# A two-layer decoder trunk: feed-forward stages entered by halves of the tokens

## The chip, the cores and the metric

The kernel runs on one core of a Trainium2 chip. The metric is device time in microseconds. Before the change the median of three runs is 2155.39 us (2155.28 to 2158.04). One more execution was profiled; it took 2157.71 us.

## The reference

512 tokens of width 1024 pass two layers in float32. Every sub-layer reads a norm of the residual x and adds to x:

```
x = x + 1/2 * swiglu_ffn(rmsnorm(x, ffn1_norm[i]), ffn1_w_gu[i], ffn1_w_down[i])
x = x + mixer_i(rmsnorm(x, mix_norm[i]))     # i=0: RG-LRU and mLSTM ("ab"); i=1: sparse attention ("nsa")
x = x + 1/2 * swiglu_ffn(rmsnorm(x, ffn2_norm[i]), ffn2_w_gu[i], ffn2_w_down[i])
...
rmsnorm(x, g)   = x * rsqrt(mean(x*x) + EPS) * g
swiglu_ffn(x)   = (silu(x @ gate) * (x @ up)) @ w_down          # inner width D_FF = 2816
out             = rmsnorm(x, final_norm)
```

## The kernel before, in words

**Layout.** x stands transposed in eight tiles `X[0..7]` of 128 features x 512 tokens. Six stages follow each other: f0a, ab, f0b, f1a, nsa, f1b; the four named f are feed-forward stages (`ffn`, L310). Each float32 operand of TensorE is split in two, a rounded part (a copy on ScalarE, `hi`) and a remainder (a subtraction on VectorE, `lo`), and each product is three matmuls, L171 to L173 (`mm3`). Weights pass `wload` (L157 on): a DMA on SP's queue into one of two `raw` buffers, a copy into one of three `whi` (L165), a remainder into `wlo` (L166). Its instructions have a priority 90 places ahead of the program's order (`AHEAD`).

**A feed-forward stage** has 22 pairs, each 128 columns of gate and of up. Pairs 0 and 1 are done in full: 16 products of 512 tokens on the scaled but unnormed x (`prep`, L98, made by the stage before in its closing loop), with the norm's sums over features (`rms_sum`, L130) and its spread over partitions (`rms_row`, L142) in between. Then `quarters` (L240) makes the normed x (`xn`, L248), cuts it by halves of features and of tokens into B11, B12, B21, B22, and forms Q7, Q6, Q5, Q4 from them. The other 20 pairs (`pair`, L364) do seven products of a quarter instead of eight, 4 x 3 matmuls of 256 tokens each, with the weights summed alike on GpSimd (`sload`, L280 to L306; L289 to L292 are the sums, L303 and L304 copy and remainder, at a priority 230 ahead). They need three PSUM banks: `a` takes B11, then Q6, Q5 and B22 on top of each other, `e` takes Q7 and Q4, `b` B21. After each product its value is read: ScalarE L387, L389, L393, VectorE L395, L384, L380, then L374, L375, and `down` (L319) splits the result into `h`. The next product on the same bank waits for that reading. B22 of a pair is done after B11 and Q7 of the next (`left`).

After every eight pairs (the last time six) the down projection adds its eight output tiles to X (L412 to L421), 512 tokens at a time; in the last of these rounds, the closing, it calls `nxt` for each tile. The mixers close with their output projections, `out_proj` (L423) and `out_half(1)` in `nsa`. After f1b the final norm scales X and eight DMAs write it out (L1138 to L1141).

**Order.** `manual_schedule(engines=PE_ONLY)` keeps TensorE's instructions of a block as written. The other engines' queues, and tiles' places in the pools, are set by a list scheduler that takes ready instructions by priority: the place in the program less the offset given by `high_priority`. Blocks `b0` to `b16` of 2064 columns are shared by all stages under one tag each.

## Time and profile before

| | us |
|---|---|
| median of three runs | 2155.39 |
| profiled execution | 2157.71 |
| its span, first to last instruction | 2156.0 |
| TensorE busy | 2034.5 (94%) |
| VectorE busy | 1467.9 (68%) |
| ScalarE busy | 1040.1 (48%) |
| GpSimd busy | 876.8 (41%) |

PE is TensorE's matmul, PEld its weight load, DVE VectorE, ACT ScalarE, POOL GpSimd, SP the queue of the DMAs. Matmuls overlap, so one is shown longer (0.28 us for 256 columns) than the step from one start to the next. The chain that ended last lies on PE for 71% of the span and on DVE for 15%. `ps` and `pt` are PSUM tiles, `t` the tiles t1 and t2, `qB` and `qQ` the quarters of x, `r` the summed weights.

### The profile page before, as it was taken

The page shows a single profiled execution, that of the slowest core. Times are in us where ns is not written, and L with a number is a line of the kernel's source. Part 1 is how long each engine was busy: PE and PEld are TensorE (multiplying, and loading weights), DVE is VectorE, ACT ScalarE, POOL GpSimd, SP SyncE. Part 2 cuts the span into 40 slices and gives each one's busy share as a digit, 9 for nine tenths or more (in the row PEclk, how much of TensorE's full clock was granted, in tenths as well). Part 3 has the DMA queues.
Part 4 walks back from the last instruction along what each step waited for, and adds up shares of the span by engine and source line. Part 5 has one row for each costly group of instructions (what it writes and reads, how often), then busy time and mean ns, then how long its engine had stood idle before and what let it go on. Part 6 is the DMA issues. An engine that isn't in the chain of part 4 may idle for free.

```text
span 2156.0 us, 31290 instructions
## 1 busy us (share of the span) xinstructions
PE 2034.5 (94%) x12184; PEld 1772.0 (82%) x12184; DVE 1467.9 (68%) x2057; ACT 1040.1 (48%) x1876; POOL 876.8 (41%) x618
## 2 busy tenths in 40 slices
PE   6899999989997999999799999999999997999997
PEld 5789988867876989898698989877777676989896
DVE  7866847489566939576784858533777778848474
ACT  4434535355443525355452525424878754535252
POOL 6534522243222616254361625201655553526242
PEclk8899999999798999999899999999999998999998
DMA  4232322322121322323132332421000031323322
GB/s 158 69 100 97 118 74 69 103 69 79 68 98 59 108 85 98 107 89 111 51 108 88 108 93 89 126 87 70 30 21 16 31 103 59 108 88 108 93 67 76
DMA packets 75765, 182.13 MB, mean 84 GB/s; under 512 B 7393, under 2 KB 8161, under 8 KB 75617
## 3 DMA queue, kind: packets, MB, share of 16 engines
q1 hardware_dynamic: 75472, 180.06, 25.9%
q8 instruction: 95, 1.56, 0.3%
q14 instruction: 54, 0.43, 0.1%
q10 hardware_dynamic: 144, 0.09, 0.0%
HBM read 178.02 MB, written 2.10 MB: 84 GB/s over the span
## 4 chain that ended last, share of the span: by engine, by line
PE 71%; DVE 15%; issue 6%; ACT 5%; POOL 2%; DMA 1%; SPq 0%; POOLq 0%; ACTq 0%; DVEq 0%
PE ps L171 18%; PE ps L172 17%; PE ps L173 17%; PE pt L172 3%; DVE wlo L304 2%; PE pt L173 2%; PE pt L171 2%; PE px L945 2%; DVE t L375 2%; PE pt L740 2%; DVE xn L248 1%; ACT wx L303 1%; DVE wlo L166 1%; PE pt L961 1%; DVE qQ L258 1%
## 5 line engine op out<-in xcount | busy, mean ns | idle before, releaser
L289 POOL TENSOR_TENSOR r<-r,r 128x512 f32<-128x512 f32 x80 | 137.9, 1724 | 651.6 <-DMA r<-wgu 588.3
L165 ACT ACTIVATE whi<-raw 128x1024 fp32r<-128x1024 f32 (+2 forms) x180 | 176.7, 982 | 363.9 <-PE ps L172 249.3
L303 ACT ACTIVATE whi<-r 128x1024 fp32r<-128x1024 f32 x192 | 182.7, 952 | 236.1 <-PE ps L172 172.3
L304 DVE TENSOR_TENSOR wlo<-r,whi 128x1024 fp32r<-128x1024 f32 x192 | 254.6, 1328 | 54.4 <-ACT whi L303 52.6
L172 PE MATMUL ps<-h,whi 128*128 128x512 f32 x704 | 277.9, 395 | 0.0
L171 PE MATMUL ps<-h,whi 128*128 128x512 f32 x704 | 277.1, 394 | 0.0
L173 PE MATMUL ps<-h,wlo 128*128 128x512 f32 x704 | 276.6, 393 | 0.0
L419 DVE SCALAR_TENSOR_TENSOR X<-ps,X 128x512 f32<-128x512 f32 x96 | 66.4, 692 | 255.7 <-PE ps L173 255.7
L166 DVE TENSOR_TENSOR wlo<-raw,whi 128x1024 fp32r<-128x1024 f32 (+2 forms) x150 | 184.7, 1232 | 79.3 <-ACT whi L165 74.5
L304 DVE TENSOR_TENSOR wx<-r,wx 128x1024 fp32r<-128x1024 f32 (+1 forms) x128 | 185.7, 1451 | 51.2 <-ACT wx L303 49.6
L171 PE MATMUL ps<-qB,whi 128*128 128x256 f32 x576 | 166.4, 289 | 10.5 <-DVE t L380 10.5
L172 PE MATMUL ps<-qB,whi 128*128 128x256 f32 x576 | 163.8, 284 | 2.4 <-DVE qB L256 2.1
L173 PE MATMUL ps<-qB,wlo 128*128 128x256 f32 x576 | 163.3, 284 | 0.0
L303 ACT ACTIVATE wx<-r 128x1024 fp32r<-128x1024 f32 (+1 forms) x128 | 121.4, 948 | 80.8 <-PE pt L173 36.3
L172 PEld LDWEIGHTS ps<-h,whi 128*128 128x128 f32 x704 | 132.2, 188 | 31.5 <-DVE h L322 1.7
L171 PE MATMUL ps<-x,whi 128*128 128x512 f32 x368 | 154.6, 420 | 3.2 <-ACT whi L1094 3.2
L173 PEld LDWEIGHTS ps<-h,wlo 128*128 128x128 f32 x704 | 132.4, 188 | 30.7
L171 PEld LDWEIGHTS ps<-h,whi 128*128 128x128 f32 x704 | 132.2, 188 | 30.7
L112 POOL TENSOR_TENSOR acc<-acc,t 128x512 f32<-128x512 f32 x48 | 76.1, 1585 | 195.9 <-ACT t L110 190.8
L290 POOL TENSOR_TENSOR r<-r 128x512 f32<-128x512 f32 x80 | 146.1, 1826 | 17.2 <-DMA r<-wgu 17.1
L291 POOL TENSOR_TENSOR r<-r,r 128x512 f32<-128x512 f32 x80 | 150.6, 1883 | 5.8
L292 POOL TENSOR_TENSOR r<-r 128x512 f32<-128x512 f32 x80 | 147.0, 1837 | 6.1
(340 smaller groups left out, 6048.0 us busy)
## 6 DMA issues: line engine op xcount, KB each, us to landing
r<-wgu SPq DMA_DIRECT2D x80, 512.0 KB, 3.7
r<-wgu SPq DMA_DIRECT2D x160, 256.0 KB, 2.9
raw<-wd SPq DMA_DIRECT2D x64, 512.0 KB, 3.5
raw<-wd SPq DMA_DIRECT2D x32, 384.0 KB, 3.1
raw<-ab_fm SPq DMA_DIRECT2D x21, 512.0 KB, 3.3
raw<-nsa_fm SPq DMA_DIRECT2D x17, 512.0 KB, 3.3
raw<-wgu SPq DMA_DIRECT2D x14, 512.0 KB, 3.3
raw<-ab_out SPq DMA_DIRECT2D x8, 512.0 KB, 3.3
```

What stands on the lines that cost most here:

```text
L112: nc.gpsimd.tensor_add(acc, acc, sq)
L165: nc.scalar.activation(hi[:, :n], raw[:, :n], AF.Copy)
L166: (eng or nc.vector).tensor_sub(lo[:, :n], raw[:, :n], hi[:, :n].bitcast(F32))
L171: nc.tensor.matmul(ps, wh, xh, start=start, stop=False, skip_group_check=on)
L172: nc.tensor.matmul(ps, wh, xl, start=False, stop=False, skip_group_check=on)
L173: nc.tensor.matmul(ps, wl, xh, start=False, stop=stop, skip_group_check=on)
L289: nc.gpsimd.tensor_add(ra[:, 1], ra[:, 0], rc[:, 3])
L290: nc.gpsimd.tensor_add(rc[:, 1], rc[:, 0], rc[:, 3])
L291: nc.gpsimd.tensor_add(ra[:, 2], ra[:, 0], rc[:, 1])
L292: nc.gpsimd.tensor_add(rc[:, 2], ra[:, 3], ra[:, 2])
L303: nc.scalar.activation(hi[:, :m * T], src, AF.Copy)
L304: nc.vector.tensor_sub(lo[:, :m * T], src, hi[:, :m * T].bitcast(F32))
```

## The change

Stages f0b, f1a and f1b no longer start with two full pairs; their 22 pairs are all done by quarters. For that the sub-layer ahead of each closes by halves of the tokens: all eight output tiles for the first 256 tokens, then all eight for the other 256, each with its own `wload` (`closing`, `out_proj`, `out_prod`). After each half tile its square is summed (`square_half`). During the second half, after its third tile, the norm of the first half is formed and B11 and B21 with it (`mid`). The quarters of the second half are made as sums of others: Q7 from the unnormed difference times the norm's row in PSUM, Q6 from B11 and Q7, Q4 from B21 and Q6, Q5 and B22 on GpSimd (`second`). The first three pairs of such a stage run side by side, in the order written in `ffn`. f0a does three full pairs and makes its quarters the same way. The final norm is done by halves too. Readings of products get a priority of 320 (`EV`) or 160. Stages ab and nsa keep their full entry (`Rows`). The blocks of some tiles change places.

```diff
 AHEAD = 90
 SAHEAD = 230
+EV = 320
+H = T // 2
 PSB = 5
 NCMP = 31
 PE_ONLY = {mybir.EngineType.PE}
...
+        def square_half(i, t):
+            ts = slice(t * H, (t + 1) * H)
+            if i == 0:
+                nc.scalar.activation(acc[:, ts], X[i][:, ts], AF.Square)
+                return None
+            sq = tp.tile([P, T], F32, name="t2", bufs=3)[:, :H]
+            nc.scalar.activation(sq, X[i][:, ts], AF.Square)
+            if i < KT - 1:
+                nc.gpsimd.tensor_add(acc[:, ts], acc[:, ts], sq)
+            return sq
...
+        def rms_sum_half(t, sq):
+            ps = psum()
+            for c in range(2):
+                n = 2 * t + c
+                nc.tensor.matmul(ps[:, 2 * c:2 * c + 2], acc[:, n * P:(n + 1) * P], ones, start=True, stop=False)
+                nc.tensor.matmul(ps[:, 2 * c:2 * c + 2], sq[:, c * P:(c + 1) * P], ones, start=False, stop=True)
+            ms = tp.tile([P, NT], F32, name="ms")[:, :2]
+            root = tp.tile([P, NT], F32, name="root")[:, :2]
+            nc.scalar.activation(root, ps[:, 0:4:2], AF.Sqrt, scale=1.0 / D, bias=eps)
+            nc.vector.tensor_scalar(ms, ps[:, 0:4:2], 1.0 / D, EPS, op0=OP.mult, op1=OP.add)
+            rsqrt(Rcol[:, 2 * t:2 * t + 2], ms, root)
...
+            def tile(self, i, t):
+                self.sq[t] = square_half(i, t)
+                if t:
+                    self.early(i)
+            def early(self, i):
+                g, n = col(self.g, i), ng[:, PRM[self.g] + i:PRM[self.g] + i + 1]
+                if i < 4:
+                    nc.scalar.activation(self.xg[:, i], X[i][:, H:], AF.Copy, scale=g)
+                else:
+                    nc.vector.scalar_tensor_tensor(self.d7[:, i - 4], X[i][:, H:], n, self.xg[:, i - 4],
+                                                   op0=OP.mult, op1=OP.add)
...
+            def split(self, name, src, parts=1):
+                t = blk(self.qb[QS.index(name)], F32R, f"q{name}")
+                hi, lo = (t[:, n * 4 * H:(n + 1) * 4 * H].rearrange("p (k t) -> p k t", k=4) for n in range(2))
+                for n in range(parts):
+                    ks = slice(n * 4 // parts, (n + 1) * 4 // parts)
+                    nc.scalar.activation(hi[:, ks], src[:, ks], AF.Copy)
+                    nc.vector.tensor_sub(lo[:, ks], src[:, ks], hi[:, ks].bitcast(F32))
+                self.Q[name] = hi, lo
...
+            def first(self):
+                for i in range(KT):
+                    n = ng[:, PRM[self.g] + i:PRM[self.g] + i + 1]
+                    nc.vector.scalar_tensor_tensor((self.b11, self.b21)[i // 4][:, i % 4], X[i][:, :H], n, R[:, :H],
+                                                   op0=OP.mult, op1=OP.mult)
+                    if i == 3:
+                        self.split("B11", self.b11)
+            def mid(self):
+                with tc.high_priority(offset=60):
+                    rms_sum_half(0, self.sq[0])
+                    rms_row_half(0)
+                    self.first()
+                    self.split("B21", self.b21)
+            def second(self, row, parts):
+                f3 = blk(self.fb[2], F32, "qf3")[:, :4 * T].rearrange("p (s k t) -> p s k t", s=2, k=4)
+                q6, q4 = f3[:, 0], f3[:, 1]
+                for n in range(parts):
+                    ks = slice(n * 4 // parts, (n + 1) * 4 // parts)
+                    nc.vector.tensor_mul(self.d7[:, ks], self.d7[:, ks],
+                                         row.unsqueeze(1).to_broadcast([P, 4 // parts, H]))
+                nc.gpsimd.tensor_mul(self.xg, self.xg, R[:, H:].unsqueeze(1).to_broadcast([P, 4, H]))
+                self.split("Q7", self.d7, parts)
+                nc.vector.scalar_tensor_tensor(q6, self.b11, -1.0, self.d7, op0=OP.mult, op1=OP.subtract)
+                self.split("Q6", q6)
+                nc.gpsimd.tensor_add(self.b11, self.xg, self.b11)
+                nc.vector.scalar_tensor_tensor(q4, self.b21, -1.0, q6, op0=OP.mult, op1=OP.subtract)
+                self.split("Q4", q4)
+                nc.gpsimd.tensor_sub(self.xg, self.d7, self.xg)
+                self.split("Q5", self.b11)
+                self.split("B22", self.xg)
...
+        def closing(prod, upd, fin):
+            for t in range(2 if fin.halves else 1):
+                ts = slice(t * H, (t + 1) * H) if fin.halves else slice(0, T)
+                for i in range(KT):
+                    ps = psum()[:, :ts.stop - ts.start]
+                    prod(i, ps, ts)
+                    upd(i, ps, ts)
+                    fin.tile(i, t)
+                    if t and i == 2:
+                        fin.mid()
+        turns = [0, 0]
...
+        def quartered(w, rb):
+            ra, rc = (blk(rb[2 * (turns[1] % 2) + i], F32, f"r{i}")[:, :4 * T].rearrange("p (s c) -> p s c", s=4)
+                      for i in range(2))
+            turns[1] += 1
+            nc.sync.dma_start(ra[:, 0:4:3], w[0].rearrange("p (s c) -> p s c", s=2))
+            nc.sync.dma_start(rc[:, 3], w[1][:, :T])
+            nc.sync.dma_start(rc[:, 0], w[1][:, T:])
+            nc.gpsimd.tensor_add(ra[:, 1], ra[:, 0], rc[:, 3])
+            nc.gpsimd.tensor_add(rc[:, 1], rc[:, 0], rc[:, 3])
+            nc.gpsimd.tensor_add(ra[:, 2], ra[:, 0], rc[:, 1])
...
+        def into(jobs):
+            hi, lo = parts(len(jobs))
+            at = 0
+            for W, src, names in jobs:
+                cs = slice(at * T, (at + len(names)) * T)
+                src = src.rearrange("p s c -> p (s c)")
+                nc.scalar.activation(hi[:, cs], src, AF.Copy)
+                nc.vector.tensor_sub(lo[:, cs], src, hi[:, cs].bitcast(F32))
+                for name in names:
...
+            def load(self, w, rb):
+                with tc.high_priority(offset=SAHEAD):
+                    q = quartered(w, rb)
+                    for names in (("B11", "Q7"), ("Q6", "B21"), ("Q4", "Q5"), ("B22",)):
+                        if names[0] not in self.W and names[-1] not in self.W:
+                            into([(self.W, q[names if len(names) > 1 else names[0]], names)])
+                return self
...
+            def p1(self):
+                self.a, self.t1 = psum(), tp.tile([P, T], F32, name="t1", bufs=3)
+                self.product(self.a, "B11", True)
+                with tc.high_priority(offset=EV):
+                    nc.scalar.activation(self.t1[:, :H], self.a[:, :H], AF.Copy)
+            def p2(self):
+                b = psum()
+                self.product(b, "B21", True)
+                with tc.high_priority(offset=EV):
+                    nc.vector.tensor_add(self.t1[:, :H], b[:, :H], self.t1[:, :H])
+                nc.scalar.activation(self.t1[:, :H], self.t1[:, :H], AF.Silu, scale=-1.0)
+            def p7(self):
+                self.e, self.t2 = psum2(), tp.tile([P, T], F32, name="t2", bufs=3)
+                self.product(self.e, "Q7", True)
+                with tc.high_priority(offset=EV):
+                    nc.scalar.activation(self.t2[:, H:], self.e[:, :H], AF.Copy)
+            def p6(self):
+                self.product(self.a, "Q6", False)
+                with tc.high_priority(offset=EV):
+                    nc.scalar.activation(self.t2[:, :H], self.a[:, :H], AF.Copy)
+            def p4(self):
+                self.product(self.e, "Q4", False)
+                with tc.high_priority(offset=EV):
+                    nc.vector.tensor_add(self.t2[:, :H], self.e[:, :H], self.t2[:, :H])
+            def p5(self):
+                self.product(self.a, "Q5", False)
+                with tc.high_priority(offset=EV):
+                    nc.vector.tensor_add(self.t2[:, H:], self.a[:, :H], self.t2[:, H:])
+            def p3(self):
+                self.product(self.a, "B22", False)
+                with tc.high_priority(offset=EV):
+                    nc.scalar.activation(self.t1[:, H:], self.a[:, :H], AF.Silu, scale=-1.0)
+                with tc.high_priority(offset=EV // 2):
+                    nc.vector.tensor_mul(self.t2, self.t1, self.t2)
+                    self.down(self.t2)
...
+                start, at, wait = 3, 19, []
+                for j in range(start):
...
+                    if j == 1:
+                        for i in range(KT):
+                            quarters.early(i)
+                        quarters.first()
+                        for args in wait:
+                            j, t2 = hidden(*args)
+                            downs(j)(t2)
+                        wait.clear()
+                j, t2 = hidden(*wait[0])
+                quarters.split("B21", quarters.b21)
+                quarters.second(R[:, H:], 1)
+                downs(j)(t2)
+            else:
+                start = 3
+                pairs = {j: Pair(Q, downs(j)) for j in range(start)}
+                for p, j in ((pairs[j], j) for j in range(start)):
+                    hi, lo = wload(wgu[j, 0])
+                    p.W["B11"], p.W["B21"] = (hi[:, :T], lo[:, :T]), (hi[:, T:], lo[:, T:])
+                p0, p1, p2 = pairs.values()
+                with tc.high_priority(offset=SAHEAD):
+                    q0, q1 = quartered(wgu[0], rb), quartered(wgu[1], rb)
+                    for name in ("Q7", "Q6", "Q4", "Q5", "B22"):
+                        into([(p0.W, q0[name], (name,)), (p1.W, q1[name], (name,))])
+                    q2 = quartered(wgu[2], rb)
+                    for names in (("Q7", "Q6"), ("Q4", "Q5"), ("B22",)):
+                        into([(p2.W, q2[names if len(names) > 1 else names[0]], names)])
                 with tc.manual_schedule(engines=PE_ONLY):
+                    p0.p1()
+                    p0.p2()
+                    with tc.high_priority(offset=EV):
+                        rms_sum_half(1, quarters.sq[1])
+                    p1.p1()
+                    p1.p2()
+                    with tc.high_priority(offset=EV):
+                        row = rms_row_half(1)
+                        quarters.second(row, 2)
+                    p2.p1()
+                    p2.p2()
+                    for f in (p0.p7, p1.p7, p0.p6, p1.p6, p0.p4, p1.p4, p0.p5, p1.p5, p2.p7, p0.p3, p2.p6, p1.p3,
+                              p2.p4, p2.p5):
+                        f()
+                left = [p2.p3]
...
+                    for j in range(max(start, j0), j1):
+                        p = Pair(Q, downs(j)).load(wgu[j], rb)
+                        end = j == j1 - 1
+                        p.p1()
+                        p.p7()
+                        for f in left:
+                            f()
+                        p.p6()
+                        p.p2()
+                        if end:
+                            p.p5()
+                            p.p4()
+                            p.p3()
+                        else:
+                            p.p4()
+                            p.p5()
+                        left = [] if end else [p.p3]
...
+            closing(out_prod, lambda i, ps, ts: nc.vector.tensor_add(X[i][:, ts], ps, X[i][:, ts]), fin)
...
+            def tile(self, i, t):
+                ts = slice(t * H, (t + 1) * H)
+                self.sq[t] = square_half(i, t)
+                nc.vector.tensor_scalar(X[i][:, ts], X[i][:, ts], col("final_norm", i), None, op0=OP.mult)
+            def put(self, t):
+                ts = slice(t * H, (t + 1) * H)
+                rms_sum_half(t, self.sq[t])
+                ps = rms_row_half(t)
+                for i in range(KT):
+                    if i in (2, 4, 6):
+                        nc.gpsimd.tensor_mul(X[i][:, ts], X[i][:, ts], R[:, ts])
+                    else:
+                        nc.vector.tensor_mul(X[i][:, ts], X[i][:, ts], ps)
+                    nc.sync.dma_start(out[:, i, ts], X[i][:, ts])
+            def mid(self):
+                self.put(0)
...
+        qb = tuple(range(7))
+        lay = ((7, 8, 9, 10), (13, 14, 15, 16), (11, 12))
+        quarters = Quarters(plan["f0a"], qb, (10, 9, 8))
+        rows = Rows(plan["ab"], 0)
+        ffn(a["wgu"][0], a["wd"][0], x, quarters, lay, rows, first)
+        quarters = Quarters(plan["f0b"], qb, (10, 9, 8))
+        ab(rows.x, quarters)
+        following = Quarters(plan["f1a"], qb, (10, 6, 8))
+        ffn(a["wgu"][1], a["wd"][1], None, quarters, lay, following)
+        rows = Rows(plan["nsa"], 0)
+        ffn(a["wgu"][2], a["wd"][2], None, following, lay, rows)
+        quarters = Quarters(plan["f1b"], (4, 5, 6, 7, 14, 15, 16), (13, 12, 3))
+        nsa(rows.x, quarters)
+        end = Output()
+        ffn(a["wgu"][3], a["wd"][3], None, quarters, ((2, 3, 12, 13), (8, 9, 10, 11), (0, 1)), end)
+        end.put(1)
```

## Rows read from the trace of the kernel before

**Rows 1.** The page, part 1: busy time, share of the span, instructions.

```profile
PE 2034.5 (94%) x12184; PEld 1772.0 (82%) x12184; DVE 1467.9 (68%) x2057; ACT 1040.1 (48%) x1876; POOL 876.8 (41%) x618
```

**Rows 2.** Waits of TensorE, whole span: us in total, times, longest.

```profile
PE ps L171 <- DVE t L380: 22.7, 37, 1.8
...
PE pt L171 <- ACT qQ L254: 20.4, 7, 4.6
```

**Rows 3.** Stretches: busy time (instructions) of each engine, clock, DMA share, GB/s.

```profile
986.00:1019.20 33.20, 33.20 (x146) 27.05 (x145) 19.13 (x24) 18.30 (x26) 8.98 (x6) 1.00 0.31 95
644.70:668.70 24.00, 24.00 (x114) 19.81 (x112) 13.86 (x18) 8.14 (x10) 4.64 (x2) 1.00 0.15 44
1087.30:1098.68 11.38, 11.38 (x99) 11.38 (x97) 9.76 (x11) 6.34 (x11) 8.40 (x5) 1.00 0.34 116
596.40:644.70 48.30, 46.85 (x200) 37.82 (x199) 27.82 (x37) 22.09 (x32) 14.70 (x9) 0.96 0.31 101
596.40:751.10 154.70, 139.47 (x815) 123.94 (x814) 113.73 (x125) 73.84 (x110) 65.81 (x36) 0.92 0.26 84
986.00:1124.50 138.50, 124.50 (x763) 111.95 (x762) 103.42 (x112) 70.09 (x104) 60.65 (x33) 0.94 0.27 84
1742.30:1873.60 131.30, 115.76 (x722) 102.58 (x721) 107.88 (x118) 69.88 (x107) 65.42 (x37) 0.92 0.29 94
45.70:129.80 84.10, 65.94 (x505) 64.13 (x504) 75.33 (x72) 44.83 (x69) 46.76 (x26) 0.86 0.24 77
1169.00:1250.70 81.70, 80.29 (x673) 79.47 (x672) 67.51 (x69) 45.88 (x78) 55.85 (x32) 1.00 0.34 111
683.00:687.00 4.00, 4.00 (x21) 4.00 (x20) 4.00 (x4) 0.26 (x1) 2.76 (x3) 0.50 0.02 8
```

**Rows 4.** Quarters: VectorE remainder (min/median/max ns); ScalarE copy (busy us, mean ns).

```profile
L258 DVE TENSOR_TENSOR qQ<-qs,qQ x16: 1210/1748/2299, 56.4 to 1814.6; 128x1024 fp32r<-128x1024 f32 x16
...
L254 ACT ACTIVATE qQ<-qs 128x1024 fp32r<-128x1024 f32 x16 | 16.8, 1050 | 10.4 <-POOL qs L266 5.2 <-POOL qs L271 5.2
```

**Rows 5.** Timeline near 660 us: start us, us, engine, operation, count.

```profile
660.51 3.40 DVE L248 SCALAR_TENSOR_TENSOR xn<-X,prm,R 128x512 f32<-128x512 f32 x5 [1.04 <-ACT R L148]
...
663.17 3.55 DVE L248 SCALAR_TENSOR_TENSOR xn<-X,prm,R 128x512 f32<-128x512 f32 x2
...
663.33 2.84 POOL L266 TENSOR_TENSOR qs<-xn 128x1024 f32<-128x1024 f32 x1 [14.48 <-DVE xn L248]
```

**Rows 6.** Timeline of VectorE in the output projection: two remainders of one buffer.

```profile
612.39 1.22 DVE L166 TENSOR_TENSOR wlo<-raw,whi 128x1024 fp32r<-128x1024 f32 x1 [0.18 <-ACT whi L165]
...
618.04 1.25 DVE L166 TENSOR_TENSOR wlo<-raw,whi 128x1024 fp32r<-128x1024 f32 x1 [0.29 <-ACT whi L165]
```

**Rows 7.** DMA issues: count, KB each, median us to landing.

```profile
raw<-ab_out SPq DMA_DIRECT2D x8, 512.0 KB, 3.3
...
raw<-wd SPq DMA_DIRECT2D x32, 384.0 KB, 3.1
...
raw<-nsa_out SPq DMA_DIRECT2D x16, 256.0 KB, 2.7
```

**Rows 8.** ScalarE copy and VectorE remainder of a 768-column weight tile.

```profile
L165 ACT ACTIVATE whi<-raw 128x768 fp32r<-128x768 f32 x32 | 27.1, 847 | 43.0 <-PE ps L172 24.9 <-issue 12.2 <-PE pt L172 4.0
...
L166 DVE TENSOR_TENSOR wlo<-raw,whi x8: 957/958/1945, 982.2 to 1016.2; 128x768 fp32r<-128x768 f32 x6, 128x1024 fp32r<-128x1024 f32 x2
```

**Rows 9.** Waits of TensorE from 668.7 to 751.1 us.

```profile
PE pt L171 <- ACT qQ L254: 5.0, 2, 2.8
...
PE ps L171 <- DVE t L380: 2.2, 3, 1.3
```

**Rows 10.** Waits of TensorE from 1169 to 1251 us.

```profile
PE ps L171 <- DVE t L380: 1.4, 3, 0.7
```

**Rows 11.** Timeline of the end.

```profile
2139.97 0.69 DVE L419 SCALAR_TENSOR_TENSOR X<-ps,X 128x512 f32<-128x512 f32 x1 [2.23 <-PE ps L173]
...
2148.16 4.48 SPq L1141 DMA_DIRECT2D out_dram<-X  x8
```

More of the change, by code (lines that the diff above doesn't have):

```diff
@@ L48, with build @@
 NPRM = _prm_columns()
-def build(tc, a, out, stages=("f0a", "ab", "f0b", "f1a", "nsa", "f1b")):
+def build(tc, a, out):
     nc = tc.nc
@@ L351, in ffn @@
-            Q, steps = quarters(qb, hb[1:4])
-            for n, f in enumerate(steps):
-                f()
-                if n in (4, 6):
-                    hidden(*wait.pop(0))
-            def product(ps, W, name, start):
-                wh, wl = W[name]
-                xh, xl = Q[name]
-                for k in range(4):
-                    ks = slice(k * P, (k + 1) * P)
-                    mm3(ps[:, :H], wh[:, ks], wl[:, ks], xh[:, k], xl[:, k], start and k == 0, k == 3, not start)
@@ L1098, in piece @@
                     nc.sync.dma_start(X[i], a["xT"][:, i])
-                prep(i, plan[stages[0]], x, False)
+                prep(i, plan["f0a"], x, False)
         nc.sync.dma_start(X[0], a["xT"][:, 0])
@@ L1103, in build @@
             piece(n)
[L1104 removed]
+        first = [w[1:] for w in w0]
         for i in range(KT):
             square(i)
[L1107 to L1133 removed]
```

323 lines of the change are left out of this document (126 added, 197 removed).

## The prediction, made before the changed kernel ran

> **What bounds the kernel now.** First the busy times: TensorE is busy for 94% of the span [rows 1], so only what it does, or waits for, can move the end. Second the waits of TensorE [rows 2]: the largest is the wait of the product B22 for VectorE's `t L380`, 22.7 us in 37 pieces; the next is for ScalarE's quarters, 20.4 us in 7 pieces. The first is spread over all feed-forward stages, the second sits where such a stage is entered. Third the stretches [rows 3], from which the prices of TensorE's work come. A product of 512 columns: 33.2 us for 144 (two of the 146 began earlier) = 0.2306 us. A product of 256 columns: 11.38 us for 96 (three of the 99 began earlier) = 0.1185 us, so two halves cost 0.237, 3% over a whole. A full pair is 48 x 0.2306 = 11.1 us, a pair by seven quarter products 84 x 0.1185 = 9.95 us. The two full pairs with the norm's sums took 24.0 us, so the sums take 1.9 us.
>
> What a stage entry loses is the stretch less this work. f0b, from the first product of the output projection to the end of pair 7: 154.7 - 192 x 0.2306 (44.3) - 24.0 - 6 x 9.95 (59.7) = 26.7 us, of which 48.3 - 44.3 = 4.0 lie at the head of the projection. f1a: 138.5 - 33.2 - 24.0 - 59.7 = 21.6. f1b: 131.3 - 22.1 - 24.0 - 59.7 = 25.5; I leave 3 of these to the end of attention, since f1a has no such head. f0a, six pairs after its two full ones: 84.1 - 59.7 = 24.4. Together 98 us, in stretches whose granted clock is 0.86 to 0.94 while the steady one has 1.00.
>
> **The change, part by part.** (1) *Work of TensorE.* f0b, f1a and f1b do 22 pairs by quarters instead of 20: each gets 2 x 9.95 + 1.9 in place of 24.0, 2.2 us less. The closing products are done twice at half width: 384 x 0.1185 - 44.3 = +1.2 for f0b, 288 x 0.1185 - 33.2 = +0.9 for f1a, 192 x 0.1185 - 22.1 = +0.7 for f1b. f0a gets one more full pair, +1.1.
>
> (2) *Entry stalls of f0b, f1a, f1b.* The first half's norm, B11 and B21 are made beside the closing's second half. After the last closing product TensorE has six products (8.5 us) that need only these, and two small sums. Then each quarter must be ready two products (2.8 us) after the one before it, because they now form a chain: Q6 from Q7, Q4 from Q6. A link is a VectorE sum (1.21 at least), a ScalarE copy (1.05) and a VectorE remainder (1.21 to 2.30, median 1.75) [rows 4]: 3.5 to 4.6 us, late by 0.7 to 1.8 at Q6 and again at Q4. Blocking decides between the ends: an `xn` of VectorE, 0.68 us each in the five before, took 2.9 us while GpSimd's 2.84 us `L266` ran beside it [rows 5]. The change puts three GpSimd operations of that size into each entry (scale xg, sum to Q5, difference to B22), and the weight sums of two more pairs. I take 1.2 at Q7 (half of a blocked remainder), 1.8 at Q6, 1.8 at Q4, 2.2 for Q5 and the late weights of pair 2, and 2 for the half clock that follows: 9 us each. Ends: 2 (0.7 twice, and 0.6 at Q7) and 20 (all of today's).
>
> (3) *Closings by halves.* Each weight tile is loaded, copied and split twice, through two `raw` buffers. One buffer's cycle is the load, the copy, the remainder: 618.04 - 612.39 = 5.65 us for 512 KB [rows 6], with a load of 3.3 [rows 7], so 2.8 us per tile against 24 x 0.1185 = 2.8 of products: level. For 384 KB 3.1 + 0.85 + 0.96 + 0.1 = 5.0, 2.5 per tile [rows 7, 8] against 18 x 0.1185 = 2.1. For 256 KB 2.7 + 0.6 + 0.65 (halves of the 512 KB times) + 0.1 = 4.05, 2.0 per tile against 1.4. Over 16 tiles, less the five that can be ready ahead (three split, two loaded): 0, 11 x 0.4 = 4, 11 x 0.6 = 7 us. VectorE has the first half's norm, two splits and three more weight tiles in the same stretch; I add 1 to 2. So 2 (f0b), 5 (f1a), 8 (f1b), 4 (the last stage, which has no quarters to make). Ends: nothing, where the delay only covers VectorE's work of (2), and twice as much.
>
> (4) *f0a.* The third full pair gives TensorE 11.1 us while the quarters are made; but VectorE does the same work and is busy for 75.3 of these 84.1 us [rows 3], so I take 11 us of the 24.4 to remain (ends 3 and 20).
>
> (5) *Evictions ahead of weights.* B22 accumulates into the bank that `L380` reads; VectorE took it behind remainders of weights and of `h`. `L380` itself is 0.41 us. Two products (2.8 us) lie between Q5 and the B22 that waits, room for one blocked remainder and the eviction. Of the 22.7 us, 8.4 lie in the four entry stretches (2.2 in f0b's [rows 9]; 2.5, 2.4 and 1.3 in the others, rows of the same form) and are in (2) and (4); 14.3 remain, and I take 11 of them. Ends: 0 (the eviction still finds a blocked remainder under way and the weights come later) and 14.3. What is put behind, the weights' remainders, has cover: in a steady stretch TensorE waits for none of them, `L380` is its only wait [rows 10]. I count 1 us more in each entry stretch for what stays.
>
> (6) *The end.* From the last update (2139.97) to 2156.0 the tail is 16 us [rows 11]. Half of the tokens leave it, so the update, the square, the sums and the first multiplication each halve; but eight DMA issues remain, 4.5 us, and a landing. I take 3 off (ends 0 and 5); with (1) and (3), 0.9 + 4 - 3 = 1.9, say 2 later.
>
> **Sum.** Gains: f0b 26.7 - (4.0 + 9 + 2 + 1) + 2.2 - 1.2 = 11.7; f1a 21.6 - (9 + 5 + 1) + 1.3 = 7.9; f1b 25.5 - (3 + 9 + 8 + 1) + 1.5 = 6.0; f0a 24.4 - 11 - 1.1 = 12.3; evictions 11; end -2. Together 46.9. The profiled execution took 2157.7 us, 1.7 of it outside the span, so the changed one would take 2110.8; the median of the runs is 2.3 below it: **2108.5 us**.
>
> One rule speaks against (3). The row: at half clock (0.50) a product of 256 columns costs 4.00 / 19 = 0.21 us [rows 3], and the clock fell after TensorE had waited; in the closing of f1a, where it never waited, it stayed at 1.00. [...] By the rows' mechanism, should it hold for all four closings, their 1152 products would cost 1152 x (0.2105 - 0.1185) = 106 us more and the time would be 2214. The waits that I forecast, 0.6 us a tile at most, are shorter than those after which the rows show a fall (up to 2.8 us a piece, [rows 9]), so I give it little.
>
> **Rivals.** *A, the entries close.* The chain keeps up because the closing's delay lets VectorE finish early: entries 3 us, closings 1, 2, 4 and 2, f0a 5, evictions 13, end 1 earlier: 19.7 + 17.9 + 17.0 + 18.3 + 13 + 1 = 87, so 2068. For: only a quarter's link is late, by about 1 us unblocked. Against: blocked operations are the median there, not the exception.
>
> *B, VectorE is the bound.* It is busy for 113.7, 103.4 and 107.9 us in the three entry stretches [rows 3] and gets eight more weight remainders in each closing, up to 8 x 1.22 = 10 us; TensorE's work there comes to 127, 116 and 104. If VectorE cannot be filled beyond 90%, then with 10 us more f0b takes 123.7 / 0.9 = 137, f1a 126 and f1b 131, so at best 17, 12 and nothing is gained; with entries of 15, closings half as long again, f0a at 15 and evictions 8, the gain is 5 + 0 - 4 + 8 + 8 - 3 = 14: 2141.
>
> *C, slower: the two `raw` buffers.* Place: the four closings, 64 tiles. If GpSimd blocks each remainder (1.95, the longest of [rows 8]) and one blocked operation stands ahead of it, a cycle is 3.1 + 0.85 + 1.95 + 1.95 + 0.1 = 8.0 us, 4.0 per tile, 1.9 over the products: 64 x 1.9 = 122 in place of the 19 counted: 2211. It turns the sign from (47 + 19) / 64 = 1.0 us per tile on. Against: in the closing of the projection the remainders ran unblocked.
>
> *D, the priorities don't do what they say:* term (5) is 0, the rest stands: 2119.
>
> **How the numbers follow.** Forecast 0.43 (its own range 2088 to 2130), A 0.23, B 0.17, D 0.06, C 0.07, the clock 0.04. The ends of all terms together reach from 2052 to 2185; leaving out two in ten gives 2068 to 2143. A measurement here tells 0.2%, 4.3 us, from no change. Slower: C and the clock, with a little of B, 0.12; the same: the rest of B's edge, 0.04; faster 0.84.
>
> **What would show it.** Right: the wait for `t L380`'s successor falls from 22.7 to under 10 us; first blocks of eight pairs run to about 91 us of stretch in f0b and f1a; the changed closing of nsa shows TensorE waiting for `wlo` or `whi` for 5 to 10 us; waits on the quarters shrink from 20.4 but stay. Wrong: closings at a granted clock of 0.5 (the rule), TensorE waiting over 1 us per tile in them (C), or VectorE busy throughout an entry stretch (B); no wait above 1 us on a quarter (A).

## The result, and the profile after

The changed kernel took 2175.39 us (median of four, 2173.21 to 2179.97) against 2156.72 for the kernel before beside it: ratio 1.0087 (1.0065 to 1.0109), 0.9% slower, outside the predicted range on its upper side. Its profiled execution took 2173.21, with a span of 2171.5; the one before took 2157.71 [rows 1]. Where 46.9 us were to be gained, these two executions show 15.5 lost.

Busy times and the largest waits of TensorE in the changed kernel (page, part 1; then us in total, times, longest):

```profile
PE 2026.6 (93%) x12964; PEld 1801.3 (83%) x12964; DVE 1493.3 (69%) x2183; ACT 1074.9 (50%) x1986; POOL 919.3 (42%) x666
```

```profile
PE ps L207 <- DVE t L453: 30.3, 25, 3.0
PE ps L208 <- DVE qQ L302: 16.4, 4, 5.2
PE ps L209 <- DVE wlo L202: 11.1, 18, 1.7
PE ps L207 <- ACT whi L201: 7.7, 8, 2.7
```

`t L453` is the reading of Q5 that was `t L380` [rows 2]; its wait grew from 22.7 us to 30.3, in fewer and longer pieces. VectorE's remainders of the quarters (`qQ L302`) cost 16.4 us in four pieces, one per feed-forward stage. Most of the waits for `wlo` and `whi` (9.0 of 11.1 us and 5.0 of 7.7) lies in the closings.

The stretches, as in [rows 3] (closing and entry of f0b, of f1a and of f1b, five quarter pairs of f0a, a steady block, the end):

```profile
581.77:637.15 55.38, 49.31 (x403) 47.52 (x402) 43.85 (x64) 28.99 (x46) 17.57 (x15) 1.00 0.46 145
637.15:739.83 102.68, 87.37 (x687) 85.10 (x685) 86.14 (x90) 53.94 (x91) 65.29 (x36) 0.95 0.34 105
973.16:1014.06 40.90, 37.57 (x303) 35.91 (x301) 30.08 (x51) 24.57 (x42) 10.95 (x12) 1.00 0.44 131
1014.06:1120.77 106.71, 89.78 (x686) 87.51 (x685) 88.74 (x93) 54.70 (x92) 67.02 (x37) 0.91 0.33 107
1741.44:1775.69 34.25, 26.77 (x194) 23.58 (x192) 26.22 (x49) 20.73 (x39) 14.58 (x14) 1.00 0.45 147
1775.69:1880.71 105.02, 91.29 (x685) 89.27 (x685) 87.47 (x94) 56.09 (x94) 63.90 (x37) 0.90 0.31 101
58.07:125.71 67.64, 55.39 (x422) 54.02 (x420) 50.55 (x51) 33.14 (x53) 40.81 (x21) 0.87 0.29 94
1165.91:1246.83 80.92, 79.12 (x674) 78.68 (x672) 65.48 (x69) 46.00 (x78) 53.33 (x31) 1.00 0.32 105
2114.16:2171.50 57.34, 42.22 (x314) 40.34 (x312) 35.59 (x69) 21.31 (x38) 15.85 (x18) 0.86 0.43 128
```

The first block of f0b takes 102.7 us for 81.5 of products and sums. The reason stands in the queues of VectorE and GpSimd (start, us, engine, operation, idle time before it):

```profile
651.18 3.37 DVE L333 SCALAR_TENSOR_TENSOR qf<-qf,qf 128x1024 f32<-128x1024 f32 x1
654.48 5.64 DVE L302 TENSOR_TENSOR qQ<-qf,qQ 128x1024 fp32r<-128x1024 f32 x3
```

```profile
651.10 2.38 POOL L332 TENSOR_TENSOR qf<-qf,qf 128x1024 f32<-128x1024 f32 x1 [3.06 <-DVE qf L330]
653.55 3.21 POOL L335 TENSOR_TENSOR qf<-qf 128x1024 f32<-128x1024 f32 x1
```

`L333`, the sum to Q4, takes 3.37 us beside GpSimd's `L332`. Behind it comes Q6's remainder, the first of the three `L302`: it too takes 3.37, beside GpSimd's `L335`, and the other two 1.21 each. TensorE has waited for it since 652.7. TensorE's two largest waits in this block:

```profile
PE ps L208 <- DVE qQ L302: 5.2, 1, 5.2
PE ps L207 <- DVE t L453: 5.2, 3, 2.7
```

### The profile page after: what moved, and what is told of

It is laid out like the page before. It is cut to its first block, busy times and chain, and to the rows that moved or that the text cites. A ratio compares the mean times of both kernels' runs of the same rounds, so it can differ in the third digit from the quotient of the medians.

```text
span 2171.5 us, 33410 instructions
## 1 busy us (share of the span) xinstructions
PE 2026.6 (93%) x12964; PEld 1801.3 (83%) x12964; DVE 1493.3 (69%) x2183; ACT 1074.9 (50%) x1986; POOL 919.3 (42%) x666
## 4 chain that ended last, share of the span: by engine, by line
PE 70%; DVE 15%; ACT 5%; issue 5%; DMA 3%; POOL 2%; SPq 0%; POOLq 0%; DVEq 0%; ACTq 0%
PE ps L207 17%; PE ps L209 17%; PE ps L208 17%; PE pt L208 3%; PE pt L209 3%; PE pt L207 3%; DVE wlo L202 2%; DVE wx L396 2%; PE px L1123 2%; PE pt L918 2%; DMA raw<-wd 2%; ACT whi L201 1%; DVE wlo L396 1%; DVE t L460 1%; PE pt L1139 1%
## 5 line engine op out<-in xcount | busy, mean ns | idle before, releaser
L380 POOL TENSOR_TENSOR r<-r,r 128x512 f32<-128x512 f32 x85 | 138.9, 1634 | 652.1 <-DMA r<-wgu 605.5
L201 ACT ACTIVATE whi<-raw 128x1024 fp32r<-128x1024 f32 (+2 forms) x211 | 202.3, 960 | 346.2 <-PE ps L208 227.1
L396 DVE TENSOR_TENSOR wlo<-r,whi 128x1024 fp32r<-128x1024 f32 (+1 forms) x207 | 269.1, 1305 | 65.5 <-ACT whi L395 60.5
L395 ACT ACTIVATE whi<-r 128x1024 fp32r<-128x1024 f32 (+1 forms) x207 | 189.7, 921 | 227.0 <-PE ps L208 145.6
L207 PE MATMUL ps<-h,whi 128*128 128x512 f32 (+1 forms) x800 | 295.0, 369 | 5.5 <-ACT whi L201 3.5
L209 PE MATMUL ps<-h,wlo 128*128 128x512 f32 (+1 forms) x800 | 294.9, 369 | 2.5 <-DVE wlo L202 2.5
L208 PE MATMUL ps<-h,whi 128*128 128x512 f32 (+1 forms) x800 | 294.2, 368 | 1.0 <-DVE h L478 1.0
L202 DVE TENSOR_TENSOR wlo<-raw,whi 128x1024 fp32r<-128x1024 f32 (+2 forms) x181 | 217.1, 1202 | 99.0 <-ACT whi L201 93.1
L586 DVE SCALAR_TENSOR_TENSOR X<-ps,X 128x512 f32<-128x512 f32 (+1 forms) x112 | 68.6, 614 | 238.3 <-PE ps L209 238.1
L207 PE MATMUL ps<-qB,whi 128*128 128x256 f32 x636 | 183.7, 289 | 22.8 <-DVE t L453 20.1
L208 PE MATMUL ps<-qB,whi 128*128 128x256 f32 x636 | 180.1, 283 | 0.0
L207 PEld LDWEIGHTS ps<-h,whi 128*128 128x128 f32 x800 | 151.7, 190 | 32.7 <-ACT whi L201 4.3
L208 PEld LDWEIGHTS ps<-h,whi 128*128 128x128 f32 x800 | 151.8, 190 | 28.8 <-DVE h L478 3.3
L383 POOL TENSOR_TENSOR r<-r 128x512 f32<-128x512 f32 x85 | 155.2, 1825 | 6.3
L207 PEld LDWEIGHTS ps<-qB,whi 128*128 128x128 f32 x636 | 122.3, 192 | 27.4 <-DVE t L453 23.7
L395 ACT ACTIVATE wx<-r 128x1024 fp32r<-128x1024 f32 (+1 forms) x136 | 124.0, 916 | 29.4 <-PE ps L209 18.9
```

What stands on the lines that cost most here:

```text
L201: nc.scalar.activation(hi[:, :n], raw[:, :n], AF.Copy)
L202: (eng or nc.vector).tensor_sub(lo[:, :n], raw[:, :n], hi[:, :n].bitcast(F32))
L207: nc.tensor.matmul(ps, wh, xh, start=start, stop=False, skip_group_check=on)
L208: nc.tensor.matmul(ps, wh, xl, start=False, stop=False, skip_group_check=on)
L209: nc.tensor.matmul(ps, wl, xh, start=False, stop=stop, skip_group_check=on)
L380: nc.gpsimd.tensor_add(ra[:, 1], ra[:, 0], rc[:, 3])
```

## The experiments

Ratios are to the kernel before, run beside each. The table gives lengths in us between first products, read from the traces ("blocks": the blocks of pairs and down products of all four feed-forward stages behind each stage's first block). Stage ab, which no edit touches, took 188.5 to 191.0 in nine traces and 193.8 to 196.6 in eight; that stayed unexplained and is left out of the comparison of stretches. Each column is one execution, and executions of one kernel lie up to 17 us apart (the kernel before: 2150.2 to 2167.2), so a difference of a few us in a long stretch is not firm.

| | before | changed | sums of x | no prior. | three | full | full, VectorE | changed, VectorE | before, VectorE |
|---|---|---|---|---|---|---|---|---|---|
| f0a to its first down product | 129.8 | 125.7 | 117.7 | 125.5 | 121.0 | 122.0 | 116.7 | 115.0 | 120.4 |
| f0b closing | 48.3 | 55.4 | 55.2 | 54.7 | 55.0 | 45.9 | 45.4 | 52.8 | 45.2 |
| f0b first block | 106.4 | 102.7 | 97.3 | 97.3 | 96.0 | 98.1 | 97.1 | 90.8 | 100.5 |
| f1a closing | 33.2 | 40.9 | 40.3 | 40.3 | 40.6 | 33.0 | 32.5 | 40.9 | 33.1 |
| f1a first block | 105.2 | 106.7 | 103.9 | 100.5 | 100.4 | 99.4 | 97.0 | 93.4 | 100.2 |
| nsa with f1b's closing | 376.5 | 389.8 | 389.4 | 390.2 | 388.9 | 381.4 | 380.4 | 386.9 | 376.0 |
| f1b first block | 106.5 | 105.0 | 101.2 | 99.3 | 100.6 | 105.1 | 100.4 | 98.4 | 106.2 |
| blocks | 1004.8 | 998.9 | 1000.0 | 997.1 | 998.4 | 1000.3 | 977.7 | 975.0 | 988.4 |
| last closing to end | 49.5 | 57.3 | 57.6 | 58.1 | 50.4 | 49.5 | 49.0 | 57.3 | 49.8 |

**Sums of x: two of GpSimd's to VectorE.**

```diff
-                nc.gpsimd.tensor_add(self.b11, self.xg, self.b11)      # L332
...
-                nc.gpsimd.tensor_sub(self.xg, self.d7, self.xg)        # L335
+                nc.vector.tensor_add(self.b11, self.xg, self.b11)      # behind Q4's remainder
                 self.split("Q5", self.b11)
+                nc.vector.tensor_sub(self.xg, self.d7, self.xg)
```

> The two sums of GpSimd in `second` (B11 for Q5, L332, and B22, L335) go to VectorE, behind Q4's remainder. In the changed kernel VectorE's Q4 sum (3.37 us, beside L332's 2.38) and Q6's remainder (3.37, beside L335's 3.21) take 3.37 instead of 1.21, and TensorE then waits 5.5, 5.5 and 4.4 us for Q6 in f0b, f1a, f1b. Theory 1, the chain is blocked by GpSimd: Q6's wait falls to 1 to 1.5 us, the half clock behind it (2 us) goes too, f0a gains 2 to 4: together 12 to 20 us, about 2158. Rival, VectorE's work is the bound: it gets 2.4 us more in each entry, what Q6 gains is lost at pair 2's and 3's weights: 0 +- 4 us, about 2175. Rival 3, the order alone: Q4's sum stands ahead of Q6's remainder anyway, the wait falls only by the blocked time of one of them: 2 us an entry, about 2168.

Ratio 1.0011 (0.9997 to 1.0025): 16 us less than 1.0087 stands for. The same links of f0b's chain (the sum to Q4, then Q6's remainder), and TensorE's waits in its first block:

```profile
645.59 1.21 DVE L332 SCALAR_TENSOR_TENSOR qf<-qf,qf 128x1024 f32<-128x1024 f32 x1
646.72 1.21 DVE L302 TENSOR_TENSOR qQ<-qf,qQ 128x1024 fp32r<-128x1024 f32 x1
```

```profile
PE pt L207 <- ACT whi L395: 4.7, 1, 4.7
PE ps L207 <- DVE t L453: 2.1, 2, 1.9
PE pt L208 <- DVE qQ L302: 1.3, 1, 1.3
PE ps L208 <- DVE qQ L302: 0.9, 1, 0.9
```

Theory 1 holds. Q6's wait fell from 5.2 to 0.9; part of it went into pair 2's weights (4.7), whose sums wait for a free set of `r` (GpSimd stood up to 13.8 us before the load into it had come).

**The last closing whole.** `Output.halves = False`, the norm's sums, row and multiplications over 512 tokens as before the change.

> The last closing and the final norm are done whole again, as before the change; all else as changed. From the last closing's first product to the end the changed kernel takes 57.3 us, the one before 49.6. Theory: the second pass over the weights and the clock that fell to half in it cost these 7.7 us, so 2175 - 7 to 8 = 2167.5. Rival, the norm of the first half (sums, its multiplications and DMA issues in front of weights' remainders on VectorE and SP) costs it and the whole tail gives it back on the other side: 2 to 4 us, 2172.

The last stretch fell from 57.3 to 50.3, the 7.0 expected; the ratio, 1.0070 (1.0053 to 1.0086), shows 4 of them. In the trace the blocks of pairs, which this edit does not touch, took 1004.9 in place of 998.9: a difference of 6 us in that row alone tells nothing.

**No priorities.** `high_priority(offset=EV)` and `EV // 2` in `Pair` become offset 0.

> The priorities of the readings of the pairs' products are taken away (offset 0), in all four feed-forward stages; the entry's own sums keep theirs. Theory 1 (the prediction's term 5, as far as the steady blocks bore it out: six blocks of eight or six pairs gained 0.7 us each): 5 to 10 us slower, 2182. Rival D, the priorities do nothing here, since the remainder that stands ahead of a reading is already under way: 0 +- 3, 2175. Rival 3, they harm: weights come later behind them, and without them it is 3 to 8 us faster, 2169.

Ratio 1.0018 (1.0006 to 1.0031): 15 us faster, in the three first blocks (5.4, 6.2, 5.7), with the blocks behind them as they were (998.9 and 997.1). Rival 3 in sign, though its place is the entries. VectorE's waits for TensorE's products, whole span, in the changed kernel and in this one:

```profile
DVE t L448 <- PE pt L209: 10.1, 8, 2.7
DVE t L431 <- PE ps L209: 7.4, 10, 2.3
DVE t L453 <- PE ps L209: 6.6, 12, 1.0
```

```profile
DVE t L431 <- PE ps L209: 5.6, 10, 1.3
DVE t L448 <- PE pt L209: 3.3, 4, 1.0
DVE t L453 <- PE ps L209: 2.4, 6, 0.9
```

24.1 us fell to 11.3: with the readings put ahead in its queue VectorE stood 12.8 us longer before them, until the product was done. In the first blocks of f0b and f1b these waits fell by 5.5 and 7.8 us, as much as the blocks gained or more; in f1a's only by 0.6, so what made that one 6.2 shorter is not shown.

**One load per closing.** In the closings' second half `wload` is left out and the last tile of the first half used.

> In the second half of each of the four closings no weights are loaded, copied or split: all eight tiles use the last tile of the first half, so the output is not the reference's. It prices the second load of the weights. Theory 1, the closings by halves are bound by their weights: TensorE's waits there (9.3, 6.2, 13.9 and about 8 us in the four) fall to 2 to 4 each, and the entries' first weights come earlier: 20 to 30 us, 2150. Rival, the norm, B11 and B21 on VectorE in the second half are what is late: waits stay near the sums of the norm, and the entries keep theirs: 5 to 10 us, 2168.

0.9990 (0.9978 to 1.0001), 21 us less: closings 1.4, 4.2 and 6.8 shorter, the end 8.6, while f1b's first block took 5.2 longer. Theory 1, but a closing by halves stays longer than a whole one (f1a 36.7 against 33.2).

**Three edits together**, on the changed kernel.

> The three edits tried one by one, together: two sums of GpSimd on VectorE (alone 16 us less than the changed kernel), last closing and final norm whole (alone 7.0 in its stretch), no priorities on the readings of the pairs (alone 15). Theory, three separate causes: 38 us less than the changed kernel, 2157 x 1.0087 - 38 = 2138, ratio 0.991. Rival, the first and the third mend the same stall (whatever frees VectorE early lets pair 2's weights come in time): 7 + 18 to 22, 2148, ratio 0.996.

0.9974 (0.9956 to 0.9991), 24 us of the 38: the rival. First blocks are 96.0, 100.4 and 100.6, hardly better than by either edit alone.

**The kernel before with the priorities.** L374 to L395 of the kernel before under the same offsets.

> The kernel before with the priorities of the change (320 and 160) on the readings of its pairs and nothing else. It is term 5 of the prediction alone. The prediction's step: 11 us less, ratio 0.995. Theory now (removing them from the changed kernel left its steady blocks as they were and made its entries 17 us shorter): the steady blocks gain nothing, and since the quarters of before are not made beside the pairs' readings the harm is small too: 0 +- 4 us, ratio 0.998 to 1.002. Rival, the harm is everywhere: a reading ahead in VectorE's queue makes it wait for TensorE while weights lie ready: 5 to 15 us more, ratio 1.003 to 1.007.

0.9996 (0.9982 to 1.0011): the priorities gave nothing.

**Full entries.** f0b, f1a and f1b close whole and do three full pairs like f0a; the blocks are placed as before the change.

```diff
-        quarters = Quarters(plan["f0b"], qb, (10, 9, 8))
-        ab(rows.x, quarters)
+        rows2 = Rows(plan["f0b"], 0)
+        ab(rows.x, rows2)
+        quarters = Quarters(plan["f0b"], (4, 5, 6, 0, 1, 2, 3), (10, 9, 8))
...
```

> As the run with the three edits, but f0b, f1a and f1b are entered as f0a is: their closings are whole, three pairs are done in full, and the quarters are made beside them as sums of others. It tells what entering by halves itself costs. Theory, the closings by halves cost 7.1, 7.7 and 9.5 us in f0b, f1a, f1b and the entry gains nothing for it: a first block of eight pairs takes 35.2 (three full pairs and sums) + 59.3 (five pairs, as f0a with VectorE's sums) = 94.5 us, about what the entry by halves has with the edits; so 20 to 25 us less than the run with the three edits, ratio 0.98. Rival, the halves pay: with full pairs first the quarters' chain stands at the same place as before and the first block takes 104: 5 to 10 us more than the run with the three edits.

0.9868 (0.9842 to 0.9894), 23 us less than the three edits, as the theory has it: closings 9.1, 7.6 and 7.5 shorter, first blocks 2.1 longer, 1.0 shorter and 4.5 longer. The same done to the changed kernel alone:

> The change with one part undone: f0b, f1a and f1b close whole and are entered by three full pairs, as f0a is; sums on GpSimd, priorities and the last closing by halves stay as changed. Theory: the halves are what made the change slower. Closings give back 9.5, 7.9 and 9 us (as the run with the three edits and full entries showed), the first blocks take what f0a's way takes with GpSimd's sums, 35.2 + 67.6 = 103 us, so 102.7, 106.7 and 105 become 103 each: together 28 to 32 us less than the changed kernel, ratio 0.995. Rival: the chain with GpSimd in it and the priorities are the cause, and without halves the entries are as long as closings and entries were together: 0 to 10 us less, ratio 1.005.

1.0006 (0.9992 to 1.0020), 17 us less, between the two. Closings gave back 9.5, 7.7 and 8.8, but f1b's first block took 110.3, and the blocks behind the first grew by 10. Full entries with two full pairs instead of three, on the three edits:

> As the run with the three edits and full entries, but with two full pairs at each of the four entries, as before the change, in place of three. TensorE has 11.1 - 9.95 = 1.1 us less work per entry, and 11.1 us less cover while the quarters are made. Theory 1, the third pair is what the gain of the entries comes from: the stall grows by most of a full pair, 6 to 9 us in each of the four: 24 to 36 us more, ratio 1.00. Rival, the gain comes from the quarters made as sums and their chain on VectorE: the stall grows by at most 2 to 3, 0 to 8 us more, ratio 0.987 to 0.991.

0.9948 (0.9934 to 0.9962), 17 us more than with three: first blocks 7.1, 7.2 and 2.9 longer, f0a 5.7. That is between theory 1's 24 to 36 and the rival's 0 to 8: the third pair does give cover, though less than theory 1 has it.

**Halves with one load**, on the three edits.

> The run with the three edits, entries by halves, but no weights are loaded in the second half of the three closings by halves: the last tile of the first half serves for all, so the output is not the reference's. With the chain mended, what do halves cost beside full entries when their weights are free? Theory, the second load explains the 24 us between the two ways: closings 2, 4 and 7 us shorter and the entries' first weights earlier by 2 to 3 each: 18 to 22 us less than the run with the three edits, ratio 0.988. Rival, half tiles cost beside their weights, by the norm's work on VectorE in the second half: 8 to 12 us less, ratio 0.993.

0.9951 (0.9934 to 0.9968), 5 us less: neither, nearer the rival. Closings 1.5, 3.5 and 8.1 shorter, f1b's first block 4.5 longer.

**No sums of weights** (L380 to L383), on the full entries.

> As the run with the three edits and full entries, but GpSimd makes no sums of weights (four per pair): Q7, Q6, Q5 and B22 use quarters as they were loaded, so the output is not the reference's. It prices GpSimd's work on VectorE. Remainders of weights then take 1.21 each (1.3 to 1.5 on the mean of all), and the weights come a GpSimd chain of 7 us earlier. Theory 1, blocked VectorE costs only where TensorE waits for it, in the entries: 5 to 8 us in each of the four, 2 us in all steady blocks: 20 to 35 us less, ratio 0.972 to 0.977. Rival, the entries are bound by the chain of the quarters, not by GpSimd: 0 to 8 us less, ratio 0.983 to 0.987.

0.9527 (0.9515 to 0.9539), 73 us less: more than either expected. VectorE's remainders of weights in a steady block of the changed kernel, then in this one (busy us, mean ns):

```profile
L396 DVE TENSOR_TENSOR wlo<-r,whi 128x1024 fp32r<-128x1024 f32 x13 | 18.5, 1426 | 6.2 <-ACT whi L395 6.0
L396 DVE TENSOR_TENSOR wx<-r,wx 128x1024 fp32r<-128x1024 f32 x10 | 16.7, 1666 | 5.7 <-PE ps L209 2.9 <-ACT wx L395 2.8
```

```profile
L392 DVE TENSOR_TENSOR wlo<-r,whi 128x1024 fp32r<-128x1024 f32 x13 | 15.9, 1225 | 12.1 <-ACT whi L391 11.8
L392 DVE TENSOR_TENSOR wx<-r,wx 128x1024 fp32r<-128x1024 f32 x10 | 12.2, 1223 | 11.3 <-ACT wx L391 11.2
```

This run also spares the weights their chain of sums. So the sums were given to VectorE:

```diff
-            nc.gpsimd.tensor_add(ra[:, 1], ra[:, 0], rc[:, 3])      # and the three behind it
+            nc.vector.tensor_add(ra[:, 1], ra[:, 0], rc[:, 3])
```

> As the run with the three edits and full entries, but the four sums of weights per pair are made by VectorE, 0.68 us each, in place of GpSimd. Leaving the sums out took 197 us of busy time off VectorE (1467.8 to 1271.1) although they were GpSimd's, and 73 us off the time; 76 pairs x 4 x 0.68 = 207 us, so VectorE is as busy as before (1478), with no operation held up by GpSimd in feed-forward stages. Theory 1, what counts is VectorE's busy time: the same within 8 us, ratio 0.983 to 0.991. Theory 2, what counts is the delay in the weights' chain (four sums of GpSimd take 7.3 us, of VectorE 2.7) and the operations that double in length where TensorE waits for them: 20 to 40 us less, ratio 0.968 to 0.978. Rival on the other side: the sums stand in VectorE's queue ahead of readings and remainders (a priority of 230), steady blocks become bound by it at 74.5 us of 80 and the entries longer: 10 to 30 us more, ratio 0.992 to 1.001.

2095.0 us, 0.9704 (0.9684 to 0.9725): theory 2 by its size, and the fastest of the kernels that leave nothing out. VectorE does 304 operations more than in the run on which this one builds (first line) and is busy for less:

```profile
PE 2011.9 (95%) x12040; PEld 1749.8 (82%) x12040; DVE 1467.8 (69%) x2073; ACT 1037.2 (49%) x1869; POOL 837.9 (39%) x598
```

```profile
PE 2006.8 (96%) x12040; PEld 1747.3 (84%) x12040; DVE 1444.1 (69%) x2377; ACT 1044.8 (50%) x1869; POOL 284.8 (14%) x294
```

Most of the gain lies where the prediction's step 5 had sought it: the blocks behind the entries fell from 1000.3 to 977.7, and TensorE's wait for the reading of Q5 almost vanished, with no priorities in either run:

```profile
PE ps L207 <- DVE t L453: 31.8, 38, 2.9
```

```profile
PE ps L207 <- DVE t L453: 4.1, 10, 0.7
```

**The same edit in the change and in the kernel before.** The change with both sorts of sums on VectorE, halves and priorities kept; and the kernel before with its sums of weights (L289 to L292) on VectorE.

> The change with halves and priorities kept, but with no sum of weights and no sum to Q5 or B22 on GpSimd: VectorE makes them. In the run without halves, sums on VectorE gave 33 us. Theory 1, GpSimd was the cause in the entries: the change now shows what it was meant to, 16 (the two sums) + 35 us less than the changed kernel, 2125, ratio 0.985, and less than the kernel before with the same edit. Theory 2, halves cost in themselves: their closings stay 7 to 9 us longer and their entries as long as others, so it stays 15 to 25 us behind the kernel before with the same edit.

> The kernel before with one edit: VectorE makes the four sums of weights per pair (80 pairs) in place of GpSimd. By the run without halves (33 us less) and its stretches: 0.6 to 1.2 us per block of pairs without an entry, 1 to 5 in each entry: 25 to 35 us less, ratio 0.984 to 0.988. If halves were held back only by GpSimd, this is slower than the change with the same edit; if halves cost in themselves, it is 10 to 20 us faster than it.

The change 0.9758 (0.9736 to 0.9781), the kernel before 0.9799 (0.9782 to 0.9815). With GpSimd out of the way the change is ahead by 0.4%, so theory 1 by the order of the two. But the halves did not give that lead: they still make the three closings 8 to 11 us longer (26 together) and the first blocks 7 to 10 shorter (24 together), and the end is 7 longer; f0a is 5 and the blocks are 13 shorter. In the kernel before, too, moving the sums alone all but ends the wait of [rows 2], 22.7 us there:

```profile
PE ps L171 <- DVE t L380: 3.4, 7, 1.7
```

Both gained more than expected (71 and 43 us). TensorE's waits in f0b's first block of the change, now 90.8 us (the three largest):

```profile
PE pt L207 <- ACT whi L395: 2.9, 1, 2.9
PE pt L208 <- DVE qQ L302: 1.3, 1, 1.3
PE ps L208 <- DVE qQ L302: 0.9, 1, 0.9
```

Last, that kernel without priorities and with the last closing whole:

> The change with its sums on VectorE, without the priorities of the readings and with the last closing whole: it differs from the run with full entries and sums on VectorE (2095, ratio 0.970) only in that f0b, f1a and f1b are entered by halves. The last closing gives 7 to 8 us. If the priorities still harm with GpSimd out of the way, another 5 to 15. Theory 1, halves pay by what full pairs cost and save: closings 7.4, 8.4 and 6.5 us longer, entries 6.3, 3.6 and 2 shorter, as in the run with priorities: 10 us more than full entries before the priorities, so 2095 to 2105, ratio 0.970 to 0.976. Rival, without priorities the entries come down to 86 to 88 us and halves win: 2080 to 2090, ratio 0.964 to 0.968.

0.9769 (0.9749 to 0.9789), 14 us behind full entries: theory 1, just above its upper edge. Closings are 24 us longer than with full entries, first blocks 9 shorter. The last closing gave 7.5, yet the time stayed where it was with the priorities: outside that and ab, the stretches grew by 12 us together. The wait for `t L453` with the priorities, then without:

```profile
PE ps L207 <- DVE t L453: 3.8, 6, 1.1
```

```profile
PE ps L207 <- DVE t L453: 11.2, 17, 2.1
```

So in this pair of kernels, with GpSimd out of the way, the priorities gain some 10 us (2 by the medians, and the 7.5 that the last closing gave). That they are what this takes is not shown: the two kernels above without them wait 4.1 and 3.4 us for the same reading. With GpSimd's sums beside them the priorities gave nothing in steady blocks and harmed in entries.

## Why the prediction was wrong

The 62 us between forecast and result in the profiled executions, by the prediction's steps: first blocks of f0b, f1a, f1b 40 (11.2, 15.2, 13.5 over the 91.5 of step 2 with its 1 us), closings 10 (f1b's counted as what the stage nsa grew by, 13.3, less 0.7 of work), f0a 8, the end 6, blocks 5, less 7 in ab.

*(1) Work of TensorE:* right; f1a's 288 products of 256 columns, 34.1 us, take all but 6.8 of its closing.

*(2) Entry stalls:* this is the step that failed: "Blocking decides between the ends", and then 1.8 us at Q6. Stalls are 21.2, 25.2 and 23.5 us in place of 9 and the 1 of step 5. I priced a link with the median remainder of [rows 4], 1.75, from a chain that GpSimd covered now and then. In the change two GpSimd operations start one behind the other exactly when the chain runs, and each of the two VectorE operations ahead of Q6's product lasts 3.37: its own 1.21, measured with the two sums on VectorE, and 2.16 more beside a GpSimd operation of 2.4 or 3.2. The row for it was there, 2.9 us for an `xn` beside a GpSimd operation of 2.84 [rows 5]. Twice that excess of 2.2 on the chain, with the 0.7 by which Q6 was late unblocked, makes 5.1; it was 5.2. Q6 is 3.4 of the 11.2 us in f0b. The reading `t L453`, which the step priced only with the 1 us, cost 5.2. And the granted clock of 0.95, 0.91 and 0.90 means 10, 19 and 21 us at the half clock (in slices of 0.5 us of these blocks it is 0.50 or 1.00, and between them only at a change); at 0.21 in place of 0.1185 us a product [rows 3] that is an estimated 4.5, 8.4 and 9.2 us lost, where the step has 2. Without GpSimd's sums f0b's first block takes 90.8, close to the 91.5 forecast; f1a's 93.4 and f1b's 98.4 stay 2 and 7 above it, which no run explains.

*(3) Closings by halves:* forecast 2, 5 and 8 us beside the products; it was 5.9, 6.8 and 12.6. The mechanism (second loads) was there, 1.4, 4.2 and 6.8 of it; the other 4.5, 2.6 and 5.8 stayed without them and were not taken apart further. Rival C did not come: even 12.6 us over 16 tiles are 0.8 a tile, under its 1.0.

*(4) f0a:* 11 of the stall were to stay, 17.9 stayed; 59.3 us for the five pairs, so 9.5, with the two sums on VectorE: the same error as in (2).

*(5) Readings first:* 11 us forecast, none had from the priorities: the blocks are 6 us shorter than before, and as short without them. I named a reason among the ends (a blocked remainder already under way), and chose the other end. The runs bear it out: with the sums of weights off GpSimd, and no priorities, the wait of 22.7 us is 3.4 in the kernel before.

*(6) The end:* 2 later forecast, 7.8 measured; a whole closing gives back 7.0. Without the second load the stretch takes 48.7, so the load was the term mis-sized, 8.6 in place of 4.

Rival B had the right engine, not the mechanism: VectorE is busy for 84% of f0b's first block, without a gap from 646.9 to 661.0 us, and late because single links are long (3.37 us); without GpSimd's sums it is busy for 91% of a block 12 us shorter, so 90% was no bound. The rule on the clock, its fall after TensorE's waits [rows 3], was rightly given little: the three changed closings ahead of an entry stood at 1.00, and the last, to its last product, at 0.93. Rival A did not come (5.2 us at Q6), and D was right on the priorities alone. What I missed is that one cause, GpSimd beside VectorE, sat in steps 2, 4 and 5, so that their errors all had the same sign. It is not the whole account: in every pair of runs here that differ in the halves (and in the places of some blocks), with GpSimd's sums or without, the three closings grew by more than their first blocks shrank (24 against 9 us in the last pair), so the entry by halves itself did not pay.

## What to carry to other kernels

An engine that looks free (GpSimd, 41% busy) may not be: price work for it by what it does to the operations beside it (here 3.37 us in place of 1.21), on the chain where they are awaited. Where several terms rest on one uncertain price, let the range move them together. A priority puts a reading ahead in a queue; here it gained nothing behind the first blocks (998.9 us with it, 997.1 without) and cost 5.4 to 6.2 us in each of the three first blocks, in two of which VectorE stood 5.5 and 7.8 us longer waiting for the product. Moving GpSimd's sums to VectorE shortened TensorE's wait for the reading of Q5 from 31.8 to 4.1 us without any priority.

## What the runs showed of the hardware

GpSimd's four sums of weights per pair took 557 us of its time in the run with full entries. Without them the kernel is 73 us of 2128 shorter (the weights are then spared the sums' delay as well); they made VectorE 197 us busier (1467.8 against 1271.1) with the same 2073 operations. VectorE making them itself was busy for 173 more (1444.1), less than they cost it on GpSimd. A remainder of 1024 columns took 1.22 us with GpSimd idle, 3.37 beside its operations. `L326`, which reads PSUM and SBUF, was not held up beside GpSimd's `L328` (two in 1.28 us); the remainder behind it, 0.69 us alone, was:

```profile
645.06 0.69 DVE L396 TENSOR_TENSOR wlo<-r,whi 128x512 fp32r<-128x512 f32 x1
645.67 1.28 DVE L326 TENSOR_TENSOR qf<-qf,pt 128x512 f32<-128x512 f32 x2
646.87 1.72 DVE L396 TENSOR_TENSOR wlo<-r,whi 128x512 fp32r<-128x512 f32 x1
```

```profile
645.54 2.50 POOL L328 TENSOR_TENSOR qf<-qf,R 128x1024 f32<-128x1024 f32 x1 [7.85 <-ACT R L175]
```

All six `L326` of the changed kernel that read PSUM ran beside an `L328` and took 0.68 us each (678 to 687 ns). In the run without sums of weights, with GpSimd idle, VectorE's operations of 512 columns in SBUF alone took 0.684 to 0.693 in a steady block.
